# The running sums of a width-31 convolution: a bank of PSUM in place of a tile of SBUF

## The chip, the cores and the metric

The kernel runs on one core of a Trainium2 chip. Its time is the device time of one execution in microseconds, so fewer is better. Before the change three runs took 623.98, 625.99 and 628.57 us; the median is 625.99.

## What is computed

One encoder layer for 256 tokens of 1024 channels. After an RMSNorm, one projection feeds two mixers; their outputs are joined, projected, and added to the residual. A mixture of experts (32 experts, two for each token) and a last RMSNorm follow. The change lies in the second mixer, whose convolution runs over 31 neighbouring tokens for each of 512 channels:

```
proj = einsum(h, w_in)                     # 1024 -> 5 x 512
a_in, a_b, a_c, b_val, b_gate = split(proj)
y_a = a_b * conv3(a_c * a_in)              # first mixer
u   = b_val * sigmoid(b_gate)              # second mixer
u   = conv31(u, conv_b_w) + conv_b_bias    # depthwise, centred
y_b = silu(layernorm(u))
y   = concat(head_rmsnorm(y_a), head_rmsnorm(y_b)) ; x = x + y @ w_out
```

## The kernel before, in words

**Stages.** The first stage (to about 166 us) does the norm, the projections, both mixers, the output projection, the routing and the gathering of tokens. The second (to about 584 us) takes the experts in 16 pairs; the last handles the final columns and the norm. All weights come from HBM through one DMA queue, SP's, in the order of a list, into a ring of 22 tiles of 1 MB. A transfer is issued when its tile has been released by its last reader; SP waits in order, so one tile that is still held keeps back all later transfers. The order on every engine is the order of the program text.

**Projections.** The 512 channels of a mixer stand as four blocks of 128 channels by 256 tokens. `proj(name, b)` makes one such block in PSUM: 16 matmuls with the high parts of the weights (L293, L294), then 8 with the low parts (L298); only `proj("g", 0)` and `proj("v", 0)` use the weights whole (L289). The order is g0, v0, g1, v1, g2, v2, g3, v3, then c0 to c3, i0 to i3, b0 to b3. Their buffers in PSUM rotate over two tags of two buffers each, the v blocks and every second block after them in the tag "h": v3 needs the buffer of v1, c1 that of v2, c3 that of v3, and such a buffer is free when VectorE has read it in `val` (L342).

**High and low parts.** ScalarE casts a weight tile to its high part (`split_hi`, L261), GpSimd subtracts to get the low part (`split_lo`, L267: one TENSOR_TENSOR of 128x2048, both inputs and the output in SBUF). There are eight such subtractions for w_in and two for w_out.

**The convolution.** `val(b)` writes block b of u into a padded tile `ub` in SBUF (the profile calls it wt, as it lies in a ring tile). `conv_one(b)` is 31 instructions on VectorE. The first (L307) multiplies a shifted window of `ub` by the channel's weight and adds the bias. The other 30 (L310) each take another window, multiply by another weight from `prm`, and add to the running sum `vb[:, b]`, in place. These 31 are called taps here. `conv_b` runs at most two blocks at a time and alternates between them, a tap of the one and a tap of the other; `run_taps(n)` puts the next n into VectorE's order:

```
val(0, sg) ; run_taps(13)        # block 0 alone
val(1, sg) ; run_taps(13)        # from here two blocks take turns
val(2, sg) ; run_taps(13)
val(3, sg) ; run_taps(94 - 39)   # 55
a_out(0) ; run_taps(5) ; a_out(1) ; run_taps(7)
a_out(2) ; run_taps(8) ; a_out(3) ; run_taps(4)
a_head(2, 2) ; run_taps(200)     # the last 6, of block 3 alone
```

`a_out(b)` (L410) multiplies the result of `proj("b", b)` in PSUM by y. Between them stand `head_stat` (squares on ScalarE, sums on TensorE, L424), `a_head` (a square root on ScalarE, L428, and a reciprocal on VectorE, L429) and `a_scale` (L441, L478, L479). The means over channels (`mu`, L528, L529) need the finished sums of all four blocks. The subtraction of the mean (L545), the squares (L546, L548) and all that follows in the kernel hang on `mu`.

**PSUM.** The four accumulators acc00 to acc11 are a bank each. acc00 is taken only after the convolution (L534) for the output projection; its earlier use, transposes of x, ends before the first tap.

Of the kernel before, what the change touches and what calls it, by code (L numbers as in the profile page):

```python
# [9 lines left out]
FT = mybir.dt.float32  # L10
# [9 lines left out]
P = 128  # L20
T = 256
# [14 lines left out]
WA, WB = 3, 31  # L36
# [4 lines left out]
def encoder_kernel(ctx, tc, x, norm_mix_g, w_in, conv_a_w, conv_b_w, conv_b_bias, ln_b_g, ln_b_b,  # L41
# [3 lines left out]
    PE, V, S, G = nc.tensor, nc.vector, nc.scalar, nc.gpsimd  # L45
# [3 lines left out]
    pacc = ctx.enter_context(tc.tile_pool(name="pacc", bufs=1, space=PSUM))  # L49
# [81 lines left out]
    vb = mx.tile([P, NB, T], FT, name="vb")  # L131
    prow = vb.rearrange("p a b -> p (a b)")[0:NPR, 0:CM]
    s1 = slot("s1")
    ub = s1[:, 0:NB * (T + 2 * HALO)].rearrange("p (b t) -> p b t", b=NB)
# [166 lines left out]
    ready = [False] * NB  # L301
    prm = cst.tile([P, NB, NPR], FT, name="prm")

    def conv_one(b):
        a = vb[:, b]
        w = lambda j: prm[:, b, R_B + j:R_B + j + 1]
        V.tensor_scalar(a, ub[:, b, 0:T], w(0), prm[:, b, R_BIAS:R_BIAS + 1], op0=OP.mult, op1=OP.add)  # L307
        yield
        for j in range(1, WB):
            V.scalar_tensor_tensor(a, ub[:, b, j:j + T], w(j), a,  # L310
                                   op0=OP.mult, op1=OP.add)
            yield

    def conv_b():
        run, nxt = [], 0
        while run or nxt < NB:
            while len(run) < 2 and nxt < NB and ready[nxt]:
                run.append(conv_one(nxt))
                nxt += 1
            if not run:  # L320
                yield False
                continue
            g = run.pop(0)
            if next(g, "end") != "end":
                run.append(g)
                yield True
# [530 lines left out]
    def hidden(pr, nms=("w1", "w3"), meanwhile={}):  # L857
        c0 = pr % 2 * 2 * CAP
        for nm in nms:
            p = ps.tile([P, F], FT, name="ph", tag="h")  # L860
            for k in range(KD):
                for e in range(2):
                    if pr == 0 and nm == "w1":
                        w = tiles[nm, e, k // 2][:, k % 2]
                    elif pr == NP - 1 and nm == "w3" and k >= 4:
                        w = tiles[nm, 2 * pr + e, k // 2 - 1][:, k % 2]
                    else:
                        w = tiles[nm, 2 * pr + e, k // 4][:, k % 4]
                    PE.matmul(p[e * CAP:(e + 1) * CAP], xg[:, k, c0 + e * CAP:c0 + (e + 1) * CAP], w,  # L869
                              start=(k == 0), stop=(k == KD - 1))  # L870
                if pr == 0 and nm == "w1" and k % 2:
                    done((nm, k // 2))
                    fill()
                if k % 4 == 3 and (nm, 2 * pr, k // 4) in owner:
                    done(*[(nm, 2 * pr + e, k // 4) for e in range(2)])
                    fill()
                if k % 4 == 3 and (nm, k // 4) in meanwhile:
                    meanwhile[nm, k // 4]()
            f = fs[pr // 2][:, pr % 2]
            if nm == "w1":  # L880
                acts[pr] = wk.tile([P, F], FT, name="sl", tag="act")
                S.activation(acts[pr], p, AF.Silu, scale=f[:, 0:1])  # L882
        if "w3" in nms:
            V.scalar_tensor_tensor(acts[pr], p, f[:, 1:2], acts[pr], op0=OP.mult, op1=OP.mult)  # L884
        return acts[pr]
# [88 lines left out]
    for pr in range(NP - 2):  # L974
# [10 lines left out]
        a = hidden(pr, meanwhile={("w1", 1): mid})  # L985
# [19 lines left out]
    a = hidden(NP - 2)  # L1005
# [16 lines left out]
    a = hidden(NP - 1, ("w3",))  # L1022
# [112 lines left out]
```

## Time and profile before

| | us |
|---|---|
| median of three runs (lowest, highest) | 625.99 (623.98, 628.57) |
| the profiled execution | 623.63 |
| its span, first to last instruction | 621.9 |
| busy: TensorE / VectorE / ScalarE / GpSimd | 555.0 / 218.0 / 113.7 / 73.0 |
| of VectorE: 120 taps of L310 | 90.3 |

PE is TensorE's matmuls, DVE is VectorE, ACT is ScalarE, POOL is GpSimd, SP issues the weight transfers. The mean granted clock of TensorE is 0.952 of its full speed. A row of a timeline gives the start, the time, the engine, the line, the operation, what it writes and reads, how many instructions the row holds, and in square brackets how long the engine had stood idle before it and what ended that. Two rows can overlap by 0.1 us or so, since the next instruction begins while the end of the last is written.

### The profile page before, as it was taken

The numbers are of one execution on the slowest core, as the hardware profiler recorded it, in microseconds if no ns is written. First come the engines' busy times: TensorE is split into PE (matmuls) and PEld (weight loads), VectorE is DVE, ScalarE is ACT, GpSimd is POOL, SyncE is SP. The second block draws the span as 40 slices with busy tenths as digits, with TensorE's granted clock in tenths as the row PEclk, the third lists the DMA queues.
The fourth block names the chain that finished last, engine by engine and source line by source line (L and its number), as shares of the span: only waits on it lengthen the run. The fifth ranks groups of instructions, "written<-read, shape, count | busy, mean of one in ns | idle before, by whom it ended". The sixth has DMA issues, their size and how long they took to land. (4 is left out here: it accounts for less than half of the span.)

```text
span 621.9 us, 7346 instructions
## 1 busy us (share of the span) xinstructions
PE 555.0 (89%) x2966; PEld 300.5 (48%) x2966; DVE 218.0 (35%) x392; ACT 113.7 (18%) x230; POOL 73.0 (12%) x53
## 2 busy tenths in 40 slices
PE   6939496799899999999999999999999999999795
PEld 5939396457644533443453335345333533534253
DVE  5799999864711202120120203012010301210232
ACT  3542041445411010000101000010100100001123
POOL 1776372610000000000000000000000000000000
PEclk8977697899799999999999999999999999999998
DMA  8990091853499999999999999999999999999992
GB/s 289 346 391 4 21 393 61 338 185 127 190 416 420 421 422 419 422 421 422 422 421 421 420 422 420 420 422 421 420 422 420 421 420 422 421 423 421 374 332 83
DMA packets 48776, 218.85 MB, mean 352 GB/s; under 512 B 6061, under 2 KB 19645, under 8 KB 25956
## 3 DMA queue, kind: packets, MB, share of 16 engines
q1 hardware_dynamic: 48554, 218.28, 87.5%
q8 instruction: 24, 0.39, 0.3%
q10 hardware_dynamic: 186, 0.08, 0.0%
q14 instruction: 12, 0.10, 0.0%
HBM read 217.30 MB, written 1.05 MB: 351 GB/s over the span
## 5 line engine op out<-in xcount | busy, mean ns | idle before, releaser
L869 PE MATMUL ph<-wt 128*64 128x512 f32 x1024 | 229.7, 598 | 3.3 <-PEq L924 3.3
L869 PEld LDWEIGHTS ph<-wt 128*64 128x64 f32 x1024 | 77.2, 138 | 142.7 <-issue 133.8
L908 PE MATMUL yp<-wt,at 128*64 128x512 f32 x448 | 99.2, 595 | 7.6 <-issue 5.8
L310 DVE SCALAR_TENSOR_TENSOR vb<-wt,prm,vb 128x256 f32<-128x256 f32 x120 | 90.3, 809 | 0.9
L884 DVE SCALAR_TENSOR_TENSOR sl<-ph,fs,sl 128x512 f32<-128x512 f32 x16 | 12.0, 751 | 217.6 <-PE ph L869 217.6
L908 PEld LDWEIGHTS yp<-wt,at 128*64 128x64 f32 x448 | 34.0, 137 | 62.5 <-issue 59.5
L293 PE MATMUL pj<-xhi,whi 128*128 128x256 f32 x128 | 36.3, 313 | 21.4 <-DVE wt L342 21.4
L1071 POOL TENSOR_TENSOR wt<-x,wt 128x256 f32<-128x256 f32 x2 | 1.6, 776 | 457.9 <-DVE x L1063 457.9
L898 DVE TENSOR_TENSOR yl<-yp,yh 128x512 fp32r<-128x512 f32 x28 | 19.4, 692 | 100.5 <-ACT yh L897 100.5
L267 POOL TENSOR_TENSOR wlo<-wt,whi 128x2048 fp32r<-128x2048 f32 x10 | 47.4, 4758 | 19.6 <-ACT whi L261 11.9
L293 PEld LDWEIGHTS pj<-xhi,whi 128*128 128x128 f32 x128 | 28.3, 221 | 21.8 <-DVE wt L342 21.8
L294 PE MATMUL pj<-xlo,whi 128*128 128x256 f32 x128 | 35.8, 310 | 0.0
L897 ACT CAST yh<-yp 128x512 fp32r<-128x512 f32 x28 | 16.4, 585 | 104.5 <-PE yp L908 104.5
L882 ACT ACTIVATE sl<-ph,fs 128x512 f32<-128x512 f32 x16 | 11.0, 687 | 101.1 <-PE ph L869 101.0
L839 ACT CAST gw<-gwp 128x256 fp32r<-128x256 f32 x16 | 5.9, 372 | 125.4 <-PE gwp L837 125.4
L294 PEld LDWEIGHTS pj<-xlo,whi 128*128 128x128 f32 x128 | 28.3, 221 | 0.0
L790 PE MATMUL gp<-gt,x2h 128*128 128x256 f32 x112 | 24.3, 298 | 0.0
L919 PE MATMUL acc<-yh,gw 128*128 128x512 f32 x56 | 23.6, 421 | 0.0
L791 DVE TENSOR_TENSOR wt<-gp,g 128x512 f32<-128x512 f32 x28 | 19.4, 692 | 8.5 <-PE gp L790 8.5
L919 PE MATMUL acc<-yl,gw 128*128 128x512 f32 x56 | 22.1, 394 | 0.2 <-DVE yl L898 0.2
L790 PE MATMUL gp<-gt,x2l 128*128 128x256 f32 x112 | 22.2, 279 | 0.0
L261 ACT CAST whi<-wt 128x2048 fp32r<-128x2048 f32 x10 | 18.9, 1900 | 14.3 <-PE pj L298 12.1
(232 smaller groups left out, 507.6 us busy)
## 6 DMA issues: line engine op xcount, KB each, us to landing
wt<-in_w_dram SPq DMA_DIRECT2D x178, 1024.0 KB, 19.8
wt<-in_w_dram SPq DMA_DIRECT2D x26, 512.0 KB, 9.7
wt<-in_w_in_dram SPq DMA_DIRECT2D x10, 1024.0 KB, 9.0
wt<-in_w_out_dram SPq DMA_DIRECT2D x4, 1024.0 KB, 10.6
x<-in_x_dram SPq DMA_DIRECT2D x2, 512.0 KB, 6.2
wt<-in_w_dram SPq DMA_DIRECT2D x4, 256.0 KB, 8.2
out_dram<-x SPq DMA_DIRECT2D x3, 256.0 KB, 2.1
out_dram<-x SPq DMA_DIRECT2D x2, 128.0 KB
```

The lines of the kernel that those rows point to most:

```text
L261: S.copy(h_, w)
L267: eng.tensor_tensor(l_, w, hi[key].bitcast(FT), op=OP.subtract)
L293: PE.matmul(p, w, xhi[:, k], start=(k == 0), stop=False)
L294: PE.matmul(p, w, xlo[:, k], start=False, stop=False)
L310: V.scalar_tensor_tensor(a, ub[:, b, j:j + T], w(j), a, op0=OP.mult, op1=OP.add)
L790: PE.matmul(p[:, k], xs[:, h, 2 * q + k], g[:, h], start=(n == 0), stop=(n == 3))
L791: V.tensor_tensor(xg[:, 2 * q:2 * q + 2], p, g2[:, 2 * q:2 * q + 2, None].to_broadcast([P, 2, 4 * CAP]), op=OP.mult)
L869: PE.matmul(p[e * CAP:(e + 1) * CAP], xg[:, k, c0 + e * CAP:c0 + (e + 1) * CAP], w, start=(k == 0), stop=(k == KD - 1))
L897: S.copy(yh, p)
L898: V.tensor_tensor(yl, p, yh.bitcast(FT), op=OP.subtract)
L908: PE.matmul(pn[nh][e * CAP:(e + 1) * CAP], at[:, k, e * CAP:(e + 1) * CAP], w[:, k % 2, nh * 512:(nh + 1) * 512], start=(k == 0), stop=(k ...
L919: PE.matmul(accm[h][nh], gw[:, h], y, start=(pr == 0 and n == 0), stop=(pr == NP - 3 and n == 1))
```

## The change

The running sums of two blocks are kept in one tile `csum` of two times 256 floats, which is the bank acc00 of PSUM; block b uses half b % 2. The first tap writes there, the next 29 read and write there, and the last tap reads it and writes `vb[:, b]` in SBUF as before.

```
+    csum = []
     def conv_one(b):
-        a = vb[:, b]
+        if not csum:
+            csum.append(pacc.tile([P, 2, T], FT, name="csum", tag="acc00"))
+        a = csum[0][:, b % 2]
         w = lambda j: prm[:, b, R_B + j:R_B + j + 1]
         V.tensor_scalar(a, ub[:, b, 0:T], w(0), prm[:, b, R_BIAS:R_BIAS + 1], op0=OP.mult, op1=OP.add)
         yield
         for j in range(1, WB):
-            V.scalar_tensor_tensor(a, ub[:, b, j:j + T], w(j), a,
+            V.scalar_tensor_tensor(a if j < WB - 1 else vb[:, b], ub[:, b, j:j + T], w(j), a,
                                    op0=OP.mult, op1=OP.add)
             yield
```

No instruction is added, dropped or moved; later lines have numbers higher by 5. VectorE's order after `val(3)`, in the kernel before:

```order
L310 SCALAR_TENSOR_TENSOR vb<-wt,prm,vb 128x256 x11
L307 TENSOR_SCALAR vb<-wt,prm 128x256
L310 SCALAR_TENSOR_TENSOR vb<-wt,prm,vb 128x256 x25
L307 TENSOR_SCALAR vb<-wt,prm 128x256
L310 SCALAR_TENSOR_TENSOR vb<-wt,prm,vb 128x256 x17
L410 TENSOR_TENSOR hT<-pj,hT 128x256
```

and in the changed one:

```order
L315 SCALAR_TENSOR_TENSOR csum<-wt,prm,csum 128x256 x8
L315 SCALAR_TENSOR_TENSOR vb<-wt,prm,csum 128x256
L315 SCALAR_TENSOR_TENSOR csum<-wt,prm,csum 128x256 x2
L312 TENSOR_SCALAR csum<-wt,prm 128x256
L315 SCALAR_TENSOR_TENSOR csum<-wt,prm,csum 128x256 x22
L315 SCALAR_TENSOR_TENSOR vb<-wt,prm,csum 128x256
L315 SCALAR_TENSOR_TENSOR csum<-wt,prm,csum 128x256 x2
L312 TENSOR_SCALAR csum<-wt,prm 128x256
L315 SCALAR_TENSOR_TENSOR csum<-wt,prm,csum 128x256 x17
L415 TENSOR_TENSOR hT<-pj,hT 128x256
```

The 55 taps are the same 55; a tap now has one large input in SBUF (wt, which is `ub`) and one in PSUM. The waits differ in one thing. The framework orders any two accesses to one bank of a PSUM tile. So where two blocks take turns, a tap before waited for the end of the tap two ahead of it, its own block's; now it waits for the one straight ahead, which uses the other half of the bank.

## Rows read from the trace of the kernel before

**Rows 1.** Busy time by stretch; the last three columns are TensorE's clock, DMA share, GB/s.
```profile
46.60:75.50 28.90, 18.11 (x114) 17.91 (x115) 28.83 (x42) 4.83 (x5) 14.99 (x3) 0.74 0.01 2
75.50:165.00 89.50, 77.00 (x422) 61.93 (x422) 70.45 (x160) 38.46 (x95) 31.41 (x26) 0.87 0.59 223
165.00:584.00 419.00, 399.96 (x2027) 174.86 (x2025) 70.39 (x122) 40.22 (x80) 0.00 (x0) 1.00 1.00 415
```

**Rows 2.** Waits up to 175 us: total, times, longest (us); TensorE's and SP's.
```profile
PE pj L293 <- DVE wt L342: 21.4, 2, 12.1
...
SPq L124 <- PE pj L294: 45.4, 2, 39.8
```

**Rows 3.** Timeline of GpSimd: the subtractions of `split_lo`.
```profile
19.88 18.69 POOL L267 TENSOR_TENSOR wlo<-wt,whi 128x2048 fp32r<-128x2048 f32 x4 [10.68 <-ACT whi L261]
...
52.02 14.99 POOL L267 TENSOR_TENSOR wlo<-wt,whi 128x2048 fp32r<-128x2048 f32 x3 [7.71 <-issue]
...
121.83 4.51 POOL L267 TENSOR_TENSOR wlo<-wt,whi 128x2048 fp32r<-128x2048 f32 x1
```

**Rows 4.** All taps by their line: least, median and longest ns, first and last start.
```profile
L310 DVE SCALAR_TENSOR_TENSOR vb<-wt,prm,vb x120: 433/479/4839, 24.7 to 119.9; 128x256 f32<-128x256 f32 x120
```

**Rows 5.** Timeline of VectorE, 9.5 to 121 us.
```profile
10.49 3.23 DVE L234 SCALAR_TENSOR_TENSOR hT<-acc,g,wt 128x256 f32<-128x256 f32 x8 [1.18 <-ACT wt L232]
...
22.21 2.41 DVE L307 TENSOR_SCALAR vb<-wt,prm 128x256 f32<-128x256 f32 x1
24.66 23.05 DVE L310 SCALAR_TENSOR_TENSOR vb<-wt,prm,vb 128x256 f32<-128x256 f32 x12
...
48.68 4.44 DVE L310 SCALAR_TENSOR_TENSOR vb<-wt,prm,vb 128x256 f32<-128x256 f32 x11
53.03 0.42 DVE L342 TENSOR_TENSOR wt<-pj,wt 128x256 f32<-128x256 f32 x1
53.37 17.88 DVE L310 SCALAR_TENSOR_TENSOR vb<-wt,prm,vb 128x256 f32<-128x256 f32 x13
...
98.55 0.41 DVE L410 TENSOR_TENSOR hT<-pj,hT 128x256 f32<-128x256 f32 x1
...
105.17 0.42 DVE L410 TENSOR_TENSOR hT<-pj,hT 128x256 f32<-128x256 f32 x1 [0.53 <-PE pj L298]
...
109.99 0.42 DVE L410 TENSOR_TENSOR hT<-pj,hT 128x256 f32<-128x256 f32 x1 [0.79 <-PE pj L298]
110.33 6.97 DVE L310 SCALAR_TENSOR_TENSOR vb<-wt,prm,vb 128x256 f32<-128x256 f32 x4
117.22 0.20 DVE L429 RECIPROCAL rs<-rs 128x8 f32<-128x8 f32 x1
117.34 3.09 DVE L310 SCALAR_TENSOR_TENSOR vb<-wt,prm,vb 128x256 f32<-128x256 f32 x6
```

**Rows 6.** The page: VectorE's same operation on 512 elements, one input in PSUM.
```profile
L884 DVE SCALAR_TENSOR_TENSOR sl<-ph,fs,sl 128x512 f32<-128x512 f32 x16 | 12.0, 751 | 217.6 <-PE ph L869 217.6
```

**Rows 7.** Timeline of TensorE: ends of projections g3, b0, b1, then the means.
```profile
34.88 1.12 PE L298 MATMUL pj<-xhi,wlo 128*128 128x256 f32 x8
...
90.68 1.12 PE L298 MATMUL pj<-xhi,wlo 128*128 128x256 f32 x8
93.56 1.12 PE L298 MATMUL pj<-xhi,wlo 128*128 128x256 f32 x8
...
112.99 2.82 PE L487 MATMUL acc<-wt,hT 128*128 128x512 f32 x6
117.96 0.74 PE L441 MATMUL hb<-ident,wt 128*128 128x128 f32 x4 [2.15 <-ACT wt L433]
118.54 0.98 PE L528 MATMUL mu<-hT,onesd 128*128 128x256 f32 x2
120.48 1.22 PE L529 MATMUL mu<-vb,onesd 128*128 128x256 f32 x2 [0.96 <-DVE vb L310]
```

**Rows 8.** Timeline of ScalarE: the square root of `a_head(2, 2)`.
```profile
113.17 0.27 ACT L428 ACTIVATE rs<-hs,epst 128x8 f32<-128x8 f32 x1 [2.27 <-PE hs L424]
```

## The prediction

> **What bounds the kernel now.** I read the busy time by stages first. From 165 to 584 us the DMA share is 1.00 and TensorE is busy 399.96 of 419 us: that stage is full, and no edit on VectorE shortens it. It can only begin earlier or later, since it starts from the tokens that the first stage routes. Between 46.60 and 75.50 us, though, DMA has a share of 0.01, TensorE is busy 18.11 of 28.90 us at a clock of 0.74, and VectorE is busy 28.83 [rows 1]. The waits name the cause: TensorE stands 21.4 us in two waits for VectorE's L342, which frees a buffer in PSUM, and SP waits 39.8 us in one piece for a projection on TensorE [rows 2]. So in the first stage VectorE's order is the chain, and the question is why it is late.
>
> The timelines answer. Twelve taps take 23.05 us from 24.66, while eleven take 4.44 from 48.68 [rows 5]. GpSimd's subtractions run without a gap from 19.88 to 38.57 and from 52.02 to 67.01 [rows 3], and the slow taps stand beside them: 13 more take 17.88 from 53.37 [rows 5]. The longest tap is 4.84 us where the median is 0.479 [rows 4], and a subtraction takes 18.69 / 4 = 4.67 [rows 3]. So a tap that begins inside a subtraction is held until its end. VectorE's row between the two kinds of taps shows what is not held: L342, with one input in PSUM and one in SBUF, takes 0.42 at 53.03, inside the subtraction that began at 52.02 [rows 3, 5]. L307 at 22.21, with one large input in SBUF and its output there, was held for 2.41 [rows 5].
>
> **The change, part by part.** It touches 124 instructions, and nothing is added or moved.
>
> *The hold.* With the sum in PSUM a tap has L342's kinds of inputs, and I take it to run beside GpSimd as L342 does. L307 now writes to PSUM. I take it as free too; held once more at the very start, it would cost its 2.41 again, less 0.4: 2 us.
>
> *The step of a tap.* Where two blocks take turns, a tap now waits for the tap straight ahead. The price is in the trace: the last six taps are block 3 alone, 3.09 us; less the 0.48 that one lasts, five steps of 0.52. Taking turns, the step is 4.44 / 11 = 0.40 [rows 4, 5]. So every tap now costs 0.52 if PSUM as the place of the sum is as quick as SBUF. VectorE writes PSUM nowhere in this trace, so this price is bounded. Reading PSUM costs nothing extra: L234, the same operation with one input in PSUM, does eight in 3.23, 0.40 each [rows 5]. From below, 0.40, as though the dependence cost nothing. From above, a bank that serves reads and writes of 256 elements one after the other: 512 elements take 751 ns against 479 for 256, 0.27 more [rows 4, 6], so 0.79. I take 0.52, since reading shows no extra, and keep both ends.
>
> [...]
>
> *From the first tap to a_out(0).* Before, 22.21 to 98.55, 76.3 us [rows 5]. It holds 13 + 13 + 13 + 55 = 94 taps: 94 x 0.52 = 48.9. Three L342 each begin 0.40 after the tap ahead and let the next begin 0.34 later (53.03 to 53.37, [rows 5]), 0.74 in place of 0.52: 0.7 together. Sum 49.6, a_out(0) at 71.8, **26.7 us earlier**.
>
> Is the cover there? Projections take 2.88 us each (90.68 to 93.56), and g3 ends at 36.0 [rows 7]. val(1) now comes at 28.9 and val(3) at 43, ahead of v3 (36.0) and c3 (47.5), which need their buffers; so TensorE's two waits go. Ten more projections end b0 at 36.0 + 28.8 = 64.8, 7 us before a_out(0). GpSimd's eight subtractions, one after the other from 19.88 at 4.67, end at 57.3, before b0's low part at 63.7. SP's long wait is for the end of c3's 16 high matmuls, which came when DMA woke at 75.5 [rows 1]; they now end at about 47.5 + 2.1 = 49.6, so the transfers come some 26 us earlier too, as the rest does. Next late after the hold is VectorE itself, by the plain sum of its taps.
>
> *From a_out(0) to a_out(3).* Five taps now cost 0.12 more each: **0.5 us later**, counting the L410s. a_out(2) and a_out(3) wait 0.53 and 0.79 for TensorE [rows 5], whose chain is the same; the slower steps of the 7 and 8 taps ahead of them (some 0.3 and 0.6) fit into that idle time.
>
> *From a_out(3) to the means.* Before, 109.99 to 120.43 (117.34 + 3.09), because the four taps at 110.33 take 6.97, the longest of them beside another subtraction [rows 5]. Freed, the reciprocal waits for ScalarE's root, which ends at 113.44 [rows 8], and starts there instead of 117.22: 3.7 earlier, and so are the last taps. TensorE then binds: L487 ends at 115.81, and L441 with L528 takes 117.96 to 119.52, 1.6 [rows 7]. So L529 can start at 117.4 in the old time, not 120.48: **3.1 us earlier**.
>
> *After the means.* The squares L548 wait for GpSimd's next subtraction (121.83, 4.51 [rows 3]), and keep two inputs in SBUF. That subtraction follows `a_scale(2)` and so the same reciprocal: it moves along by 3.1 to 3.5. Everything behind moves with it: transfers into released tiles, the start of the experts, the end.
>
> The sum: 26.7 - 0.5 + 3.1 = 29.3 us. Against the profiled execution's 623.63 that is 594.3. The median of the runs, 625.99, stands 2.4 higher, so the forecast is **596.7**.
>
> **Range of the price.** The step counts 99 times, so 0.01 more costs 1 us. A step of 0.60 costs 0.08 x 99 = 7.9, and 1.4 where the idle time of TensorE's waits is used up: 606. A step of 0.40 gives back 11 us by VectorE alone, but TensorE's b0 ends at 64.8, so at most 7: 590. L307 held once: 2 more.
>
> **Rivals.**
>
> *The hold stays.* A tap still reads its window and a [P,1] weight from `prm` in SBUF. L342 has no such scalar, and L307, with one large input and two scalars, was held [rows 5]. If the scalar's read is what is held, the taps inside subtractions end when they did, but each tap outside them costs 0.52 in place of 0.40. Of the 13 taps at 53.37 three are held; the other 10, the 55 behind val(3) and 5 behind a_out(0) are 70, and 70 x 0.12 = 8 us. I take 7, since GpSimd's shorter work holds a few of them anyway. The time is 633, slower. It decides if the tap behind val(1), or any inside a subtraction, lasts over 4 us. For it: nothing in the trace joins a scalar, an input in PSUM and a subtraction. Against: a scalar is one number for each partition, and L307 also differs from L342 in writing to SBUF without an input in PSUM.
> [...]
>
> *Reads and writes share the bank.* At 0.79 a step, 99 x 0.27 = 26.7 is given back, and the 7, 8 and last 6 taps overrun TensorE's chain by some 4: 30.7 against 29.3, so 627, no change. It decides from about 0.78; beyond it the kernel is slower. Against it: L310 in SBUF reads and writes one place in each tap without that cost, but SBUF is another memory.
>
> *The gain is lost further on.* If the weights were not loaded in time, the experts would wait. From 49.6 us on DMA must bring what it brought between 75.5 and 165, 223 GB/s x 89.5 us = 20 MB [rows 1]; at 415 GB/s that is 48 us, and about 86 are there. I give this no time of its own.
>
> **Chances.** Held no more, with a step of 0.40 to 0.60: 0.78, and 590 to 606; of it 0.13 is for a step over 0.56, a slower access to PSUM, and 601 to 606. Held no more, with a step of 0.60 to 0.77: 0.07, 606 to 625, nearly all of it faster. Hold stays: 0.09, 630 to 636. A step of 0.78 or more: 0.06, 626 or above, half of it within 1%. A measurement of this kernel tells about 1% (6.3 us) from no change. So faster by over 1%: 0.83; within 1%: 0.06; slower by over 1%: 0.11. The range is 588 to 607: the forecast's own, with the runs' scatter of about 2 us.
>
> **What would show it.** After the change: no tap over 1 us beside a subtraction; steps of taps near 0.52 everywhere, the earlier ones at 0.40 too; the PE waits for val's line gone; `a_out(0)` near 72 and the second mean near 91; DMA moving again near 50; the stretch of the experts as long as before. A step near 0.6 or 0.8 puts the error into the price of PSUM, a tap of 4.5 us into the hold, and a longer stretch of experts into the loading.

## The result and the profile after

The changed kernel takes 600.0 us (median of 4 runs, 599.5 to 601.5) against 626.4 for the kernel before on the same chip (4 runs, 624.0 to 628.6): a ratio of 0.958, 95% interval 0.953 to 0.962. The forecast was 596.7. The profiled execution took 599.47 us with a span of 597.8, against 623.63 and 621.9 before.

The taps by their line (least, median, longest ns, first and last start), which answer to [rows 4]:

```profile
L315 DVE SCALAR_TENSOR_TENSOR csum<-wt,prm,csum x116: 436/490/491, 22.4 to 88.8; 128x256 f32<-128x256 f32 x116
L315 DVE SCALAR_TENSOR_TENSOR vb<-wt,prm,csum x4: 481/481/481, 47.3 to 89.3; 128x256 f32<-128x256 f32 x4
```

The longest tap is now 0.491 us; it was 4.839. GpSimd's subtractions are as long as before (18.36 / 4 = 4.59 us each, 4.67 before) and stand beside these taps (its timeline: start, us), as in [rows 3]:

```profile
19.59 18.36 POOL L267 TENSOR_TENSOR wlo<-wt,whi 128x2048 fp32r<-128x2048 f32 x4 [10.32 <-ACT whi L261]
39.38 18.41 POOL L267 TENSOR_TENSOR wlo<-wt,whi 128x2048 fp32r<-128x2048 f32 x4 [1.42 <-ACT whi L261]
```

VectorE's timeline, as in [rows 5]:

```profile
22.37 6.27 DVE L315 SCALAR_TENSOR_TENSOR csum<-wt,prm,csum 128x256 f32<-128x256 f32 x12
...
29.39 0.55 DVE L312 TENSOR_SCALAR csum<-wt,prm 128x256 f32<-128x256 f32 x1
29.98 5.74 DVE L315 SCALAR_TENSOR_TENSOR csum<-wt,prm,csum 128x256 f32<-128x256 f32 x11
...
47.27 0.48 DVE L315 SCALAR_TENSOR_TENSOR vb<-wt,prm,csum 128x256 f32<-128x256 f32 x1
...
49.42 11.52 DVE L315 SCALAR_TENSOR_TENSOR csum<-wt,prm,csum 128x256 f32<-128x256 f32 x22
...
71.92 0.42 DVE L415 TENSOR_TENSOR hT<-pj,hT 128x256 f32<-128x256 f32 x1
...
83.52 0.42 DVE L415 TENSOR_TENSOR hT<-pj,hT 128x256 f32<-128x256 f32 x1
```

Twelve taps inside subtractions take 6.27 us where twelve took 23.05. The step is (11.52 - 0.49) / 21 = 0.525 with two blocks taking turns, and (6.27 - 0.49) / 11 = 0.525 with one alone. The last tap of a block reads its sum from PSUM and writes to SBUF; the one at 47.27 stands inside a subtraction and took 0.48, so with the output in SBUF a tap isn't held either once its second large input has left SBUF. `a_out(0)` begins at 71.92, 26.6 us earlier than before.

Waits up to 150 us on TensorE (total, times, longest), and SP's over the whole span, as in [rows 2]. No wait for `val` (now L347) is left, and SP's longest for a projection falls from 39.8 to 13.0:

```profile
PE hs L429 <- ACT wt L425: 6.2, 2, 3.7
PE va L557 <- DVE hT L553: 3.7, 1, 3.7
```

```profile
SPq L124 <- PE pj L294: 14.3, 2, 13.0
```

The second of TensorE's waits leads to what the forecast missed. TensorE's timeline from the second mean matmul on, then VectorE's first addition of the squares and GpSimd's subtraction beside it:

```profile
89.82 0.70 PE L534 MATMUL mu<-vb,onesd 128*128 128x256 f32 x2
90.35 3.60 PE L492 MATMUL acc<-wt,hT 128*128 128x512 f32 x8
97.63 1.01 PE L557 MATMUL va<-onesd,hT 128*128 128x1 f32 x4 [3.68 <-DVE hT L553]
...
100.78 3.62 PE L492 MATMUL acc<-wt,hT 128*128 128x512 f32 x4
104.19 1.98 PE L577 MATMUL hs<-hsel,wt 128*128 128x2 f32 x16
```

```profile
91.88 4.30 DVE L553 TENSOR_TENSOR hT<-hT 128x256 f32<-128x256 f32 x1
```

```profile
91.39 4.51 POOL L267 TENSOR_TENSOR wlo<-wt,whi 128x2048 fp32r<-128x2048 f32 x1
```

In the kernel before, the same eight matmuls and the wait behind them (second mean at 120.48):

```profile
121.50 5.57 PE L487 MATMUL acc<-wt,hT 128*128 128x512 f32 x8
128.06 0.60 PE L552 MATMUL va<-onesd,hT 128*128 128x1 f32 x4 [1.00 <-DVE hT L548]
```

In the changed kernel eight matmuls take 3.60 us at 90.35; four of the same line take 3.62 at 100.78, half the speed. The windows show the granted clock (third column from the right, then DMA share and GB/s):

```profile
46.60:75.50 28.90, 23.18 (x193) 22.89 (x191) 27.08 (x57) 9.38 (x20) 20.50 (x16) 0.97 0.67 259
94.00:97.60 3.60, 0.00 (x0) 0.00 (x0) 3.37 (x3) 0.00 (x0) 2.76 (x2) 1.00 1.01 387
97.60:104.40 6.80, 6.77 (x14) 3.57 (x14) 3.09 (x9) 4.65 (x8) 0.00 (x0) 0.50 0.74 298
128.70:142.00 13.30, 11.74 (x54) 10.54 (x55) 9.19 (x32) 5.43 (x12) 0.00 (x0) 0.50 0.39 164
```

The first row answers to [rows 1]: DMA moves in the stretch in which it had stood still. Then TensorE does nothing from 94 to 97.6, and at 0.50 it works at half speed until 104.4; once more from 128.7 to 142, where the tokens are routed. The second mean matmul comes 30.7 us earlier than before (120.48 to 89.82), the first expert's matmul only 25.2 (166.36 to 141.17), and the span is 24.1 shorter. So 5.5 us were gained and given back between these two. The experiments, e1 to e10, ask three things: what ended the hold, what sets the step of 0.525, and what took the 5.5 us.

### The profile page after: what moved, and what is told of

The parts are those of the page before. It is cut to its first block, busy times and chain, and to the rows that moved or that the text cites. A ratio compares the mean times of both kernels' runs of the same rounds, so it can differ in the third digit from the quotient of the medians.

```text
span 597.8 us, 7346 instructions
## 1 busy us (share of the span) xinstructions
PE 550.6 (92%) x2966; PEld 296.3 (50%) x2966; DVE 185.8 (31%) x392; ACT 114.4 (19%) x230; POOL 64.2 (11%) x53
## 3 DMA queue, kind: packets, MB, share of 16 engines
HBM read 217.30 MB, written 1.05 MB: 365 GB/s over the span
## 5 line engine op out<-in xcount | busy, mean ns | idle before, releaser
L874 PE MATMUL ph<-wt 128*64 128x512 f32 x1024 | 230.3, 598 | 3.6 <-PEq L929 3.4
L874 PEld LDWEIGHTS ph<-wt 128*64 128x64 f32 x1024 | 76.9, 138 | 144.1 <-issue 135.2
L315 DVE SCALAR_TENSOR_TENSOR csum<-wt,prm,csum 128x256 f32<-128x256 f32 x116 | 56.7, 488 | 3.8
L903 DVE TENSOR_TENSOR yl<-yp,yh 128x512 fp32r<-128x512 f32 x28 | 19.4, 692 | 100.5 <-ACT yh L902 100.5
L267 POOL TENSOR_TENSOR wlo<-wt,whi 128x2048 fp32r<-128x2048 f32 x10 | 45.8, 4609 | 11.7 <-ACT whi L261 11.7
L902 ACT CAST yh<-yp 128x512 fp32r<-128x512 f32 x28 | 16.4, 586 | 104.4 <-PE yp L913 104.4
L293 PE MATMUL pj<-xhi,whi 128*128 128x256 f32 x128 | 32.1, 287 | 0.0
L294 PE MATMUL pj<-xlo,whi 128*128 128x256 f32 x128 | 32.1, 287 | 0.0
L293 PEld LDWEIGHTS pj<-xhi,whi 128*128 128x128 f32 x128 | 25.3, 197 | 0.0
L294 PEld LDWEIGHTS pj<-xlo,whi 128*128 128x128 f32 x128 | 25.2, 197 | 0.0
L896 PE MATMUL tp<-ident,sl 128*128 128x128 f32 x64 | 12.0, 310 | 9.0 <-DVE sl L889 9.0
```

Of the source, the lines that this page charges most:

```text
L267: eng.tensor_tensor(l_, w, hi[key].bitcast(FT), op=OP.subtract)
L293: PE.matmul(p, w, xhi[:, k], start=(k == 0), stop=False)
L294: PE.matmul(p, w, xlo[:, k], start=False, stop=False)
L315: V.scalar_tensor_tensor(a if j < WB - 1 else vb[:, b], ub[:, b, j:j + T], w(j), a, op0=OP.mult, op1=OP.add)
L902: S.copy(yh, p)
L903: V.tensor_tensor(yl, p, yh.bitcast(FT), op=OP.subtract)
```

## Experiments

Where a run is compared inside the program, I use three marks of its trace: the second mean matmul (L534 in the changed kernel), the first matmul of the norm (L577) and the first expert's matmul (L874). The two differences between them leave out how early the stage began.

**e1: one block at a time, sums in SBUF.** The change did two things to a tap: one of its inputs left SBUF, and it now waits for the tap straight ahead. This run does the second without the first, on the kernel before; the order of the taps changes with it, since a block now ends before the next begins.

```
-            while len(run) < 2 and nxt < NB and ready[nxt]:
+            while len(run) < 1 and nxt < NB and ready[nxt]:
```

> The kernel before with the sums in SBUF, but one block at a time, so that every tap waits for the tap ahead, as it does with the bank of PSUM. Theory (a tap with two large inputs in SBUF is held by a subtraction of GpSimd; the waiting itself only costs 0.12 us a tap): taps inside subtractions still last up to 4.8 us, taps outside them step by 0.52 in place of 0.40, some 70 x 0.12 = 8 us, so a_out(0) near 106 and a time of 633 (628 to 637), slower than before. Rival (it was the waiting of each tap for the one ahead that ended the hold, not the place of the sum): no tap over 1 us, a_out(0) near 72, time near 600.

Measured: 633.9 us, ratio 1.012 (1.009 to 1.016). VectorE's timeline:

```profile
24.76 23.03 DVE L310 SCALAR_TENSOR_TENSOR vb<-wt,prm,vb 128x256 f32<-128x256 f32 x12
...
63.44 2.56 DVE L310 SCALAR_TENSOR_TENSOR vb<-wt,prm,vb 128x256 f32<-128x256 f32 x5
...
106.71 0.42 DVE L410 TENSOR_TENSOR hT<-pj,hT 128x256 f32<-128x256 f32 x1
```

The hold stays: the first 12 taps take 23.03 where they took 23.05. Block 0 began alone in the kernel before too, so waiting and hold stood together there already. Free taps step by (2.56 - 0.48) / 4 = 0.52, and `a_out(0)` is at 106.7. So the waiting costs 8.2 us up to `a_out(0)` and 7.5 in the medians, where 8 was priced, and it isn't what freed the taps. The step of 0.52 is the same in SBUF as in PSUM.

**e2: even blocks in PSUM, odd blocks in SBUF.** Both kinds of taps in one program.

```
-        a = csum[0][:, b % 2]
+        a = vb[:, b] if b % 2 else csum[0][:, 0]
```

> The changed kernel with only the even blocks' sums in PSUM, the odd blocks' in SBUF. Theory (each tap by its own operands): even taps last under 0.6 us everywhere, odd taps up to 4.8 inside subtractions; free steps 0.40, since the two sums no longer share a bank. The first 13 taps (block 0) run free to 29 us; then some 0.9 tap per us to the end of the subtractions near 57, and 0.40 a tap behind it: a_out(0) near 80 to 84, time 610 (604 to 618). Rival (the waiting of each tap for the one ahead ended the hold): here taps take turns without that wait, so from block 1 on all are held as before: a_out(0) over 90, time 620 to 626. Rival (an engine with any PSUM sum in flight is not held): about 594 to 600.

Measured: 614.1 us, ratio 0.980 (0.977 to 0.982). The taps by their line, and VectorE's timeline inside GpSimd's subtractions, which here run without a gap from 20.26 to 38.68:

```profile
L315 DVE SCALAR_TENSOR_TENSOR vb<-wt,prm,vb x60: 433/479/4610, 34.5 to 109.6; 128x256 f32<-128x256 f32 x60
L315 DVE SCALAR_TENSOR_TENSOR csum<-wt,prm,csum x58: 472/476/491, 23.2 to 95.4; 128x256 f32<-128x256 f32 x58
```

```profile
30.06 4.13 DVE L312 TENSOR_SCALAR vb<-wt,prm 128x256 f32<-128x256 f32 x1
34.12 0.48 DVE L315 SCALAR_TENSOR_TENSOR csum<-wt,prm,csum 128x256 f32<-128x256 f32 x1
34.51 4.44 DVE L315 SCALAR_TENSOR_TENSOR vb<-wt,prm,vb 128x256 f32<-128x256 f32 x1
```

Each tap behaves by its own operands: no tap with its sum in PSUM lasts over 0.491, those in SBUF up to 4.61, in turns and with the same kind of weight from `prm`, one number for each partition. The first tap of a block has one large input in SBUF in either kernel; with its output in SBUF too it is held (4.13), with its output in PSUM it isn't (0.55 at 29.39 above). `a_out(0)` came at 87.57, later than the 80 to 84 expected, since I had put the rate between holds too high; the time lies in its range.

**e3: two banks.** Even blocks' sums in one bank, odd blocks' in another. Two output products that need the second bank come after the means; in the changed kernel one of the two stands ahead of them.

```
-        if not csum:
-            csum.append(pacc.tile([P, 2, T], FT, name="csum", tag="acc00"))
-        a = csum[0][:, b % 2]
+        while len(csum) < 2:
+            csum.append(pacc.tile([P, T], FT, name="csum", tag=f"acc0{len(csum)}"))
+        a = csum[b % 2]
...
-    rest = [(0, 0, 0), (1, 0, 0)] + ...
+    rest = [(0, 0, 1), (1, 0, 1), (0, 0, 0), (1, 0, 0)] + ...
```

> The changed kernel with the even blocks' sums in one bank and the odd blocks' in another (the two matmuls that need the second bank come after the means). Theory (0.525 is the wait for the tap ahead, which both sums in one bank bring about): steps of 0.40 while two blocks take turns, a_out(0) then bound by TensorE's projection b0, near 64.5 to 66 in place of 71.9, second mean 6 to 8 us earlier, time 593 (589 to 597). Rival (0.525 is what PSUM takes for a tap): steps stay 0.52, a_out(0) at 72, time 599 to 602.

Measured: 588.3 us, ratio 0.939 (0.936 to 0.942), below the range expected. VectorE's timeline:

```profile
44.41 8.71 DVE L315 SCALAR_TENSOR_TENSOR csum<-wt,prm,csum 128x256 f32<-128x256 f32 x22
...
64.23 0.42 DVE L415 TENSOR_TENSOR hT<-pj,hT 128x256 f32<-128x256 f32 x1 [2.70 <-PE pj L298]
```

The step is (8.71 - 0.49) / 21 = 0.39, against 0.40 in SBUF: PSUM as the place of the sum costs a tap nothing, and the 0.525 came with the one bank that both blocks shared. That it was the order which the program keeps between two accesses of one bank, and not a limit of the bank itself, is argued and not shown: the same 0.52 stands in e1, where no bank is shared and each tap waits for the one ahead, but no run uses two halves of one bank without that order. `a_out(0)` now waits 2.70 us for TensorE, the bound that the prediction named for this case. The second mean comes at 80.90, 8.9 us earlier than in the changed kernel, more than expected: there TensorE waits 6.2 us in L429 for the squares of `a_out` (the wait shown above) and its clock is 0.50 from 73.9 to 80.2; here neither happens, and 60 to 75 us and 73.9 to 80.2 run at 1.00. The product that went behind the means doesn't explain it, since the second mean matmul waits 0.87 us for VectorE's last tap here. Behind the mean ten matmuls run in place of eight, and TensorE's wait is 2.65 us, not 3.68.

**e4: the squares' sum in PSUM.** The held additions behind the mean get the same change.

```
+    psq = ps.tile([P, T], FT, name="psq", tag="h")
...
-        S.activation(sqs[:, b], vb[:, b], AF.Square)
+        S.activation(sqs[:, b] if b else psq, vb[:, b], AF.Square)
     for b in range(1, NB):
-        V.tensor_tensor(sqs[:, 0], sqs[:, 0], sqs[:, b], op=OP.add)
+        V.tensor_tensor(psq if b < NB - 1 else sqs[:, 0], psq, sqs[:, b], op=OP.add)
```

> The changed kernel with the sum of the squares behind the mean also kept in PSUM (first square and running sum there, last sum in SBUF), so that VectorE's three additions are not held by the subtraction at 91.4. Theory (the held additions leave TensorE idle for 3.7 us, and its granted clock falls to 0.5 behind that): additions end near 93 in place of 96.2, the va matmul starts near 94 behind the running matmuls, the clock stays 1.0 there, and the first norm matmuls come at 97.5 to 98.5 in place of 104.2: 6 us earlier, of which the gather's stretch may give back up to 3; time 594 (592 to 598). Rival A (the clock falls there anyway): va near 94 but norm matmuls near 100.5, time 596.5 to 598. Rival B (gain is lost in a later wait, on DMA or VectorE): 599 to 601.

Measured: 592.9 us, ratio 0.947 (0.944 to 0.949). VectorE's and TensorE's timelines:

```profile
91.58 0.96 DVE L554 TENSOR_TENSOR psq<-psq,hT 128x256 f32<-128x256 f32 x2
92.65 0.42 DVE L554 TENSOR_TENSOR hT<-psq,hT 128x256 f32<-128x256 f32 x1
```

```profile
93.48 0.50 PE L558 MATMUL va<-onesd,hT 128*128 128x1 f32 x4
...
95.00 1.88 PE L492 MATMUL acc<-wt,hT 128*128 128x512 f32 x4
97.01 1.95 PE L578 MATMUL hs<-hsel,wt 128*128 128x2 f32 x16
```

The additions end at 93.07, the va matmuls follow the eight matmuls without a wait, and the four matmuls take 1.88 again. From the mean to the norm it takes 7.50 us in place of 14.37. Both rivals are out: the norm came at 97.0, not 100.5, and the time isn't near 599.

**e5: TensorE kept busy while it waits.** The hold stays; only the idle time is filled, by transposes that nobody reads.

```
+    idle = ps.tile([P, P], FT, name="idle", tag="h")
+    for _ in range(28):
+        PE.transpose(idle, ident, ident)
     va = ps.tile([P, 2], FT, name="va", tag="mm")
```

> The changed kernel with 28 transposes of the identity on TensorE, whose result nobody reads, between the eight matmuls behind the mean and the va matmuls: they fill the 3.7 us in which TensorE waits for the held additions of the squares. Theory (TensorE's idle time is what lowers the granted clock behind it): clock 1.0 from 90 to 104 us, va near 97.6 as before, norm matmuls near 101.2 in place of 104.2, time 597 (596 to 598.5). Rival (the clock falls there for another cause): clock 0.5 from about 97.6, norm matmuls at 104 or later, time 600 to 601.

Measured: 594.8 us, ratio 0.950 (0.947 to 0.954). TensorE's timeline:

```profile
90.87 0.70 PE L534 MATMUL mu<-vb,onesd 128*128 128x256 f32 x2
91.41 3.60 PE L492 MATMUL acc<-wt,hT 128*128 128x512 f32 x8
94.84 3.22 PE L557 MATMUL idle<-ident 128*128 128x128 f32 x28
98.71 0.61 PE L560 MATMUL va<-onesd,hT 128*128 128x1 f32 x4 [0.65 <-DVE hT L553]
...
100.34 1.88 PE L492 MATMUL acc<-wt,hT 128*128 128x512 f32 x4
102.34 1.95 PE L580 MATMUL hs<-hsel,wt 128*128 128x2 f32 x16
```

The va matmuls start 7.84 us behind the mean, as late as after the change (7.81), but the clock stays at 1.00 and the norm follows 11.47 behind the mean in place of 14.37. So of the 6.9 us between e4 and the changed kernel, 2.9 are the clock and 4.0 the hold itself. The profiled execution, 596.23, is 3.2 us below the changed kernel's 599.47, close to these 2.9. The median is 5.2 lower and lies under the range expected: two of the four runs took 593.7 and 593.9 at a mean clock of 0.98 where the profiled one shows 0.971, and no trace says where they gained it. The kernel before also stood 1.2 lower beside this run.

**e6: the waits of the routing filled in the same way.**

```
+    idle2 = ps.tile([P, P], FT, name="idle2", tag="h")
+    for _ in range(8):
+        PE.transpose(idle2, ident, ident)
     turn_x(1, 2, V.tensor_copy)
...
-    for _ in range(8):
+    for _ in range(14):
         PE.transpose(dummy, ident, ident)
```

> The changed kernel with idle time of TensorE in the routing filled in the same way: eight transposes ahead of the turn that waits 1.18 us, and 14 in place of 8 ahead of the gather. Theory (the short waits there lower the clock from 128.7 to 142): clock 1.0 through the gather, its two groups of 16 matmuls take 2.05 each in place of 3.75, first expert's matmuls some 3 us earlier, time 597 (596 to 598.5). Rival (the clock falls there whatever fills the waits): groups stay at 3.75, and the added transposes at half clock delay the gather by up to 1.2, time 600 to 601.5.

Measured: 595.6 us, ratio 0.952 (0.949 to 0.955). This lies just under the range expected. The window of the routing, at full clock:

```profile
124.00:140.00 16.00, 12.39 (x91) 9.69 (x92) 13.32 (x49) 7.88 (x20) 1.38 (x5) 1.00 0.53 198
```

From the norm to the first expert's matmul it takes 33.84 us in place of 36.98. Another 1.5 of this profile's gain lie ahead of the norm, where nothing was edited: the low clock there was shorter in this execution (0.50 for some 3.4 us from 99.9, in place of 6.8).

**Both kernels once more, one execution each,** to see which low stretches belong to the change.

> The kernel before once more, for its clock: does the granted clock behind the second mean fall in the same places in another execution? If what is given back behind the means belongs to the change, the stretch from the second mean matmul to the first expert's matmul lasts 45 to 47 us again (45.9 in the first trace), and over 50 in the changed kernel (51.4). If it is the chance of one execution, the two overlap.

> The changed kernel once more, for the same question: second mean to first expert's matmul 51.4 us in its first trace, with clock 0.5 in 97.6 to 104.4 and 128.7 to 142. If it belongs to the change, both low stretches stand there again and it lasts over 50; if chance, down to 46.

TensorE's timeline of the kernel before, second execution (625.9 us), then a window of its routing and one of the changed kernel's in its second execution (600.3 us):

```profile
119.62 1.22 PE L529 MATMUL mu<-vb,onesd 128*128 128x256 f32 x2 [0.61 <-DVE vb L310]
120.64 5.29 PE L487 MATMUL acc<-wt,hT 128*128 128x512 f32 x8
127.22 0.61 PE L552 MATMUL va<-onesd,hT 128*128 128x1 f32 x4 [1.29 <-DVE hT L548]
...
128.85 1.88 PE L487 MATMUL acc<-wt,hT 128*128 128x512 f32 x4
130.85 1.95 PE L572 MATMUL hs<-hsel,wt 128*128 128x2 f32 x16
```

```profile
154.90:168.40 13.50, 11.86 (x55) 10.89 (x56) 9.36 (x33) 5.88 (x12) 0.25 (x2) 0.50 0.42 177
```

```profile
129.70:143.00 13.30, 11.74 (x55) 10.45 (x57) 9.26 (x33) 5.37 (x11) 0.00 (x0) 0.50 0.39 164
```

In the kernel before, the eight matmuls behind the mean ran mostly at half clock (0.50 from 120.5 to 125 us in the first trace; 5.57 and 5.29 us in place of 3.60) and filled the wait: the va matmuls waited only 1.29, and what followed ran at full clock (four matmuls in 1.88). The marks of all these traces, in us:

| | mean to norm | norm to first expert |
|---|---|---|
| before, first and second | 11.21, 11.23 | 34.67, 36.96 |
| one block at a time (e1) | 11.22 | 34.76 |
| even blocks in PSUM (e2) | 11.22 | 34.75 |
| changed, first and second | 14.37, 14.30 | 36.98, 37.02 |
| two banks (e3) | 12.68 | 36.85 |
| squares in PSUM (e4) | 7.50 | 36.92 |
| wait for the squares filled (e5) | 11.47 | 36.94 |
| waits of routing filled (e6) | 12.84 | 33.84 |

The first column differs by 3.1 us in both pairs, and e1 and e2 stand with the kernel before: that belongs to the change. Its size varies, though: e6 is the changed kernel up to the norm and took 12.84, 1.6 above the kernel before.

The second column stays open. From the second mean to the first expert the kernel before took 45.9 and 48.2 us and the changed one 51.4 and 51.3, so neither of the two outcomes named ahead came out whole. In the routing the kernel before had a short low stretch in its first trace (0.50 from 156.6 to 163.0 us) and one of 13.5 us in its second. So the 2.3 us of the 5.5 that were lost there can't be put down to the change by these pairs. Nor are they shown to be the chance of one trace: e1 and e2, with 34.76 and 34.75, stand with the short stretch, while the changed kernel (twice), e3, e4 and e5 had the long one in all five traces.

**All together.** Two banks and the squares' sum in PSUM, without (e7, e9) and with (e8, e10) the transposes in the routing; e9 and e10 are the same kernels with more runs.

> Two banks for the sums and the squares' sum in PSUM together (two matmuls ahead of the squares as in the changed kernel). If the two gains add where they don't overlap: second mean at 80.9 as with two banks, va near 85.0 behind the eight matmuls at full clock, norm matmuls near 88.5 in place of 93.6 (two banks) and 97.0 (squares), time 583.5 (580 to 586). Rival (the transfers or the held squares no longer set it, and something behind does): 587 to 589.

> The same with the waits of the routing filled by transposes as well. Theory of the idle time: 3 us below the run without them, 580.5 (577 to 584). Rival (the clock falls there whatever fills the waits): same time as the run without them or up to 1.2 more.

> Two banks with the squares' sum in PSUM, timed with more rounds: 584 (582 to 586) as before; the clock falls in the routing again.

> The same with the waits of the routing filled, timed with more rounds. Theory of the idle time: 3 to 5 us below the run without them, 580 (578 to 582), and clock 1.0 through the gather. Rival: no difference.

Without the transposes: 584.6 (581.8 to 585.7) and 585.1 (581.4 to 588.1), ratio 0.936 (0.933 to 0.939) by the longer timing. With them: 581.4 (580.7 to 586.3) and 581.9 (580.9 to 584.3), ratio 0.931 (0.929 to 0.933). Each of the four medians lies in the range expected for it. Mean to norm is 7.50 in all four traces, so up to the norm the two edits add up; in time, 5.2 off the 588.3 of e3 would be 583.1, and the two medians stand 1.5 and 2.0 above that. The medians with the transposes are some 3 us lower. The intervals of the two versions still touch at 0.933, so this difference is likely and not clear of noise. The version without them scatters with the clock (581.4 us at a mean of 0.984 over the span, 588.1 at 0.969; norm to first expert 39.54 and 35.53 in its traces), and with the transposes the clock is full from 80 to 130 us and that stretch takes 34.82 and 34.72 in both traces; the window of the second:

```profile
80.00:130.00 50.00, 45.42 (x245) 30.92 (x244) 30.29 (x103) 25.90 (x69) 8.59 (x10) 1.00 0.65 243
```

This version beats the changed kernel (whose ratio to before is 0.953 to 0.962) by about 18 us.

## Why the prediction was right, point by point

- **The hold** was right, with its reason. No tap exceeds 0.491 us beside subtractions. e1 and e2 show that the place of the operands ended it, tap by tap, and neither the waiting nor the scalar matters. Inside a subtraction of e2 a tap takes 0.48 with its sum in PSUM and the next 4.44 with both large inputs in SBUF. The first tap of a block has only one, and was held too with its output in SBUF (L312, 4.13), but not with it in PSUM (0.55); why one is enough there, no run shows.
- **The step** was right: 0.525 against 0.52. Its reason, the wait for the tap straight ahead, agrees with e1 (0.52 in SBUF) and e3 (0.39 in two banks), with the limit said there. That one bank serves reads and writes in turn, the rival of 0.79, is out. The slower access to PSUM, a step over 0.56, to which the prediction gave 0.13, is shown by no run: the taps' median is 490 ns against 479, and their step 0.39 in two banks against 0.40 in SBUF. Only the first tap of a block became clearly longer in PSUM, 0.55 against 0.41, and why isn't shown.
- **a_out(0)** came at 71.92 (71.8 expected), a move of 26.6 (26.7). Its cover was there: b0 ends at 64.4 (64.8), and SP's long wait ends at 49.1 (49.6).
- **a_out(0) to a_out(3)**: 0.2 us later (0.5).
- **a_out(3) to the means**: 4.2 us earlier in the first traces (3.1). Of the 1.1 more, 0.5 is L446 with L533, which took 1.05 us at full clock and not 1.56; the L492 ahead of them ended 0.4 sooner. The second mean stands 30.7 us earlier in the first pair of traces and 28.9 in the second; 29.3 was forecast.
- **After the means** is the step that failed: "Everything behind moves with it". The subtraction did move along, and the squares were held 4.30 us (3.55 before). But TensorE's eight matmuls now ran at full clock, ended 4.1 us behind the mean in place of 6.6, and left it idle for 3.68 us; behind that its clock fell, and matmuls that had run at full speed now ran at half speed and set the time of the norm. That gave back 3.1 us in both pairs of traces, and 1.6 in e6's execution of the same instructions; e5 shows that 2.9 of it come back when the clock stays up. The forecast was 3.3 low. Between the two profiled executions it was 5.2 low: besides this, 2.3 us went in the routing, where the cause is open, and 1.1 in the experts' stretch, while the means came 1.4 earlier than forecast.
- **The experts' stretch** is nearly as long as before: from the first expert's matmul to the end of the span 456.6 us against 455.5, and 456.6 against 456.4 in the second pair. So nothing was lost there to weights that came late, beyond these 1.1 and 0.2 us.
- **Range**: its lower end rested on a step of 0.40 with TensorE's b0 as the bound, 590. Two banks made that case: 588.3. That it went below 590 is not the step alone, since the clock behind `a_out(0)` stayed up too.

## What to carry to other kernels

When VectorE's operations last as long as the GpSimd operations beside them (here 4.84 us beside 4.67), look at where their large operands lie. Here moving one running operand to PSUM freed them (0.491 at most), and two such chains were quicker in two banks than in one (steps of 0.39 against 0.525). After a gain ahead of it, price the next stage again with the clock that TensorE will then have: work that ends sooner in front of an unchanged wait becomes idle time, and the stretch behind it may run at half speed (here 3.68 us idle, then 6.8 us at 0.50). Compare marks inside several traces, those of the experiments too, before giving 2 us to the change or to chance.

## What the runs showed of the hardware that was not expected

Idle time of under 4 us cost more than its own length: 3.68 us of it were followed by 6.8 us at 0.50, and with 28 unread transposes in its place the clock stayed at 1.00 and the norm came 2.9 us sooner. In the routing, waits of 1.18, 0.71 and 0.84 us in the changed kernel came with a low stretch of 13.3 us; stretches of some 6 to 13.7 us at 0.50 stand in both traces of either kernel and in e3, e4, e5, e7 and e9, and none in the three with transposes there (e6, e8, e10: 1.00). What else decides it is open: with two banks and the squares in PSUM the clock fell near 90.7 in one trace (e7, below), though TensorE had been busy for all but 0.12 of the 9.1 us before, and not in the other trace of the same kernel (e9).

```profile
81.60:90.70 9.10, 8.98 (x38) 5.09 (x37) 5.72 (x16) 6.50 (x14) 5.99 (x4) 1.00 1.00 396
90.70:94.90 4.20, 4.20 (x13) 2.21 (x12) 1.22 (x5) 0.94 (x4) 0.00 (x0) 0.60 0.76 316
```

The hold seems to have run both ways. Two of GpSimd's short additions (L407, now L412) took 1.80 to 1.89 us beside the old taps (87.5 to 94.7 us) and 1.52 to 1.57 beside the new ones.
